# A hybrid decoder block: the first MLP product ahead of the last two norms, its operands in other room

## Chip, core and metric

The kernel runs on one core of a Trainium2 chip, as one program. The metric is the device time of an execution in microseconds. Three executions of the kernel before stand for its time, and a fourth was recorded by the profiler.

## The reference

One layer over 1024 tokens of width 1024, in float32. Its last two parts matter here:

```
x = x + concat([y_a, y_b, y_c]) @ w_out                       # three token mixers
x = x + memory_cross_attention(rms_norm(x, norm_cross), ...)  # 4 heads of 128, 256 memory rows
hm = rms_norm(x, norm_mlp) @ mlp_w1                           # 1024 -> 4096
x = x + square(relu(hm)) @ mlp_w2                             # 4096 -> 1024
```

## The kernel before

All products run on TensorE as three matmuls each: both operands are split into a high half and the rest (`split` and `split2`: a cast on ScalarE, a subtraction on VectorE), and `mm3` (L130 to L135) sums high x high (L133), high x low (L134) and low x high (L135). The program is written in order, but each engine's queue is put in order by a list scheduler that works with estimated times: an instruction that is ready by the estimate may be queued ahead of one traced before it. A queue is then fixed, and an engine runs it in that order. SP, which issues most transfers, is such a queue too. A pool hands out buffers by tag; a new tile waits for the last reader of the old tile in its bytes.

**Cross attention** runs as a software pipeline over eight tiles of 128 tokens (`for i in range(NT + 6)` in `run`): the output projection (`out_rows`, `out_b` with the tile `xr` loaded from x1_d, L1270), the norm and its transposes (`cross_h`), the query product (`cross_q`, `cross_qT`), scores and softmax (`cross_p`), values (`cross_o`), and from i = 10 `cross_w` (L1365 on), which multiplies by `wo`, adds the residual x (L1375), stores it to x3_d (L1376) and normalizes it for the MLP (square on ScalarE L1380, a ten-step reciprocal root on VectorE from L156, a multiply L196). `norm_T` transposes the normalized rows on TensorE (eight 128 x 128 transposes, L1392) and copies them into the four blocks of `h3`: `h3["gn"]` holds half g of the model width of tokens 512(n-1) to 512n-1. Tiles 4 to 7 of `cross_w` run in a loop of their own at the end, with `norm_T` two tiles behind.

**The MLP** (`mlp`) works on four groups of 1024 hidden columns. Each group has two halves, up and down, and each half is a 2 x 2 block product made from seven products instead of eight (`PRODS`, with sums of blocks from `block_sums`: S1 to S4 of the weights, T1 to T4 of the activations). A product is 4 row blocks (m) x 4 k x 3 = 48 matmuls of 128 x 512. Its weight operand `wm` is split from a raw block `wq` or a sum `wsum`, its other operand `bm` from `h3` or the sum `hsum`. In the first group `bm` is also stored to `hb_d` (L1470), and later groups load it from there. The order in the up half is 1, 2, 5, 6, 3, 7, 4. Product 1 reads w1 block "11" and `h3["11"]`, product 2 block "12" and `h3["21"]`: both are tokens 0 to 511. Product 5 needs S1 = "21" + "22" of the weights and T1 = `h3["12"]` - `h3["11"]`, so the last four tiles' norms.

What decides the order around the border of the two stages:
- `blk` has ten buffers of 8 KB per partition. It serves `xoT`, the four blocks of `h3`, the normalized rows of t = 6 and 7 (`n3y2`, one buffer), the first two raw weight blocks `wq`, `wm` of the first product, all `bm`, and later `xacc` and `am`. `blk2` has four, for other `wm`.
- The raw blocks of w1 come in 1 MB loads: two into `blk` at t = 4 (L1770), the others from the pool `mlp` (five `wq` buffers, L1479), which is opened after cross attention has closed all of its pools.
- `mlp` is a generator. `run` takes its first step (product 1 with its evictions), then `norm_T` of t = 6 and 7, then the rest.
- In the first group the weights' sums are made on GpSimd (`V if g else G`), in later groups on VectorE.
- PSUM has eight banks of 512 columns. In the cross stage four serve the query and score products (tag mg) and four the others (tag mm); `self.psum(0)` then opens a pool of eight for the MLP. A half opens four banks each for its chains ch 0, 1 and 2 (`ps[ch, m]`).
- On the right side of the memory, from the edge inwards, lie `blk2` (32 KB), `xl`, `xe`, `wr` and `xq` (called `xp` in the code); the scan and sparse attention before had there `pm` (20 KB), `woa` (42 KB) and `gdnb` (12 KB, with the scan's `oc`, stored to ya_d at L1101). `xl` holds 44 KB, `xq` 28 KB, among it `g2` and `xr`.

Of the kernel before, what the change touches and what calls it, by code (L numbers as in the profile page):

```python
# [50 lines left out]
class Block:  # L51
# [64 lines left out]
    def mm_ps(self, shape, name="mm"):  # L116
        own = self.gbanks and self.stage in ("gp", "gi", "gs", "gn", "xq", "xp")
# [1173 lines left out]
    def cross_q(self, pool, hT, wq):  # L1291
# [5 lines left out]
        qc = self.xl.tile([P, H, P], F32, name="xqc", bufs=2)  # L1297
# [7 lines left out]
    def cross_qT(self, pool, qc):  # L1305
# [4 lines left out]
        qT = [self.xl.tile([P, H, P], F32R, name=f"xqT{i}", bufs=2) for i in range(2)]  # L1310
# [28 lines left out]
    def cross_o(self, pool, Pm, v, oT, hp):  # L1339
# [5 lines left out]
        for i in range(2):  # L1345
            h = hp * 2 + i
            PT = [self.xl.tile([P, 2, 256], F32R, name=f"xPT{j}", bufs=2) for j in range(2)]
# [15 lines left out]
    def cross_w(self, x, y, t, oT, wo, g3):  # L1363
# [12 lines left out]
        nc.sync.dma_start(self.x3_d[t], x)  # L1376
# [65 lines left out]
    def mlp(self, pool, blk, h3, wq):  # L1442


        self.stage = "mlp"
# [31 lines left out]
        def raw(src):  # L1477
            t = pool.tile(bshape, F32, name="wq", bufs=5)
            nc.sync.dma_start(t, src)  # L1479
            return t  # L1480

        def new(name, tag=None):
            return lambda: early.pop(name, None) or pool.tile(bshape, F32, name=name, tag=tag or name)

        early = {"wsum": pool.tile(bshape, F32, name="wsum", tag="wsum")}

        NG = FF // GF
        for g in range(NG):

            q = dict(zip(("11", "12", "21", "22"), [raw(x) for x in self.w1_blocks(g)] if g else wq + [raw(x) for x in self.w1_blocks(0)[2:]]))  # L1490
            left = self.block_sums(V if g else G, q, {"new": new("wsum")}, False)
            right = self.block_sums(V, h3, {"new": new("hsum", "asum")}, False)
            a, ps = {}, {}
            for i, p in enumerate((1, 2, 5, 6, 3, 7, 4)):
                l, r, ch, dst = self.PRODS[p]
                l, r = half(left(l), *((blk, "blk") if g == 0 and p == 1 else ())), rows(g, i, lambda: right(r))
                for m in range(4):
# [6 lines left out]
                    for c in dst:  # L1504
                        if (c, m) not in a:
                            if m == 0:
                                a[c] = pool.tile(bshape, F32, name="aq" + c)
                            a[c, m] = x = a[c][:, m]
                            Sc.activation(x, ps[ch, m], AF.Relu if c == "21" else AF.Copy)  # L1509
                            if c == "21":  # L1510
                                V.tensor_mul(x, x, x)
                        else:
# [37 lines left out]
    def run(self):  # L1550
# [117 lines left out]
        with ExitStack() as bs:  # L1668
# [140 lines left out]
```

## Time and profile before

| | us |
|---|---|
| median of 3 executions | 1636.0 |
| lowest, highest | 1629.88, 1637.38 |
| profiled execution, its time | 1631.19 |
| span of the profiled execution | 1629.4 |
| PE busy in the span | 1508.6 (93%) |
| VectorE busy | 1171.4 (72%) |
| ScalarE busy | 739.6 (45%) |
| GpSimd busy | 318.6 (20%) |
| DMA queue on SP, share of 16 engines | 34.8% |

The span runs from the first to the last instruction in the trace; the time holds what lies around it too. PE is TensorE's matmul side, PEld its weight loads, DVE VectorE, ACT ScalarE, POOL GpSimd, SPq the queue that issues transfers. In a timeline a row gives the start, the duration, the engine, the line and the tiles written and read; in brackets stands the idle time of the engine before it and what ended that. Matmuls overlap, so the step from one start to the next, not the duration, is what one costs.

### The profile page before, as it was taken

The page shows a single profiled execution, that of the slowest core. Times are in us where ns is not written, and L with a number is a line of the kernel's source. Part 1 is how long each engine was busy: PE and PEld are TensorE (multiplying, and loading weights), DVE is VectorE, ACT ScalarE, POOL GpSimd, SP SyncE. Part 2 cuts the span into 40 slices and gives each one's busy share as a digit, 9 for nine tenths or more (in the row PEclk, how much of TensorE's full clock was granted, in tenths as well). Part 3 has the DMA queues.
Part 4 walks back from the last instruction along what each step waited for, and adds up shares of the span by engine and source line. Part 5 has one row for each costly group of instructions (what it writes and reads, how often), then busy time and mean ns, then how long its engine had stood idle before and what let it go on. Part 6 is the DMA issues. An engine that isn't in the chain of part 4 may idle for free.

```text
span 1629.4 us, 20582 instructions
## 1 busy us (share of the span) xinstructions
PE 1508.6 (93%) x7497; PEld 1256.2 (77%) x7497; DVE 1171.4 (72%) x2149; ACT 739.6 (45%) x1483; POOL 318.6 (20%) x297
## 2 busy tenths in 40 slices
PE   6999999997975789999979996999999999999999
PEld 6877788885775678888768875888888888888887
DVE  7649868678258688985767777996569656865783
ACT  4535777883541656665434542433224223323331
POOL 3021434345355333221401103100000000000000
PEclk9999999998997999999999997999999999999999
DMA  6130121221543533323712356813551364146202
GB/s 213 38 97 21 45 59 52 78 67 44 163 152 98 168 115 119 94 59 128 289 66 75 120 186 265 330 57 130 206 208 34 134 235 165 52 155 242 95 7 97
DMA packets 113811, 201.93 MB, mean 124 GB/s; under 512 B 15157, under 2 KB 64046, under 8 KB 106542
## 3 DMA queue, kind: packets, MB, share of 16 engines
q1 hardware_dynamic: 112174, 195.37, 34.8%
q0 software_dynamic: 1536, 5.24, 0.9%
q8 instruction: 59, 0.97, 0.2%
q14 instruction: 42, 0.34, 0.1%
HBM read 150.26 MB, written 50.33 MB: 123 GB/s over the span
## 4 chain that ended last, share of the span: by engine, by line
PE 65%; DVE 16%; ACT 9%; issue 5%; DMA 3%; POOL 1%; SPq 0%; ACTq 0%; DVEq 0%; POOLq 0%
PE mlp_mm L134 13%; PE mlp_mm L135 13%; PE mlp_mm L133 13%; ACT junka L588 5%; DVE acc L741 1%; PE gi_mm L1029 1%; PE xq_mm L133 1%; PE xq_mm L134 1%; PE xw_mm L135 1%; PE xw_mm L133 1%; PE xw_mm L134 1%; PE xq_mm L135 1%; DVE tk_t L596 1%; PE small_mm L135 1%; DVE junk L590 1%
## 5 line engine op out<-in xcount | busy, mean ns | idle before, releaser
L134 PE MATMUL mlp_mm<-bm,wm 128*128 128x512 f32 x448 | 178.6, 399 | 11.9 <-DVE bm L1456 11.9
L133 PE MATMUL mlp_mm<-bm,wm 128*128 128x512 f32 x448 | 178.0, 399 | 2.5 <-DVE rs_x L156 1.3
L135 PE MATMUL mlp_mm<-bm,wm 128*128 128x512 f32 x448 | 178.1, 398 | 0.0
L135 PE MATMUL mlp_mm<-wm,am 128*128 128x512 f32 x448 | 177.1, 395 | 0.0
L134 PE MATMUL mlp_mm<-wm,am 128*128 128x512 f32 x448 | 177.0, 395 | 0.0
L133 PE MATMUL mlp_mm<-wm,am 128*128 128x512 f32 x448 | 175.1, 395 | 0.0
L1455 ACT CAST wm<-wq 128x2048 fp32r<-128x2048 f32 x32 | 61.2, 1911 | 211.9 <-PE mlp_mm L134 211.7
L1545 DVE TENSOR_TENSOR xacc<-xacc,mlp_mm 128x512 f32<-128x512 f32 x112 | 75.9, 684 | 69.7 <-PE mlp_mm L135 69.7
L134 PEld LDWEIGHTS mlp_mm<-bm,wm 128*128 128x128 f32 x448 | 85.0, 190 | 33.0 <-DVE bm L1456 12.7
L133 PEld LDWEIGHTS mlp_mm<-bm,wm 128*128 128x128 f32 x448 | 85.1, 190 | 23.4 <-DVE rs_x L156 1.6
L135 PEld LDWEIGHTS mlp_mm<-bm,wm 128*128 128x128 f32 x448 | 85.1, 190 | 20.3
L133 PEld LDWEIGHTS mlp_mm<-wm,am 128*128 128x128 f32 x448 | 84.1, 188 | 20.4
L134 PEld LDWEIGHTS mlp_mm<-wm,am 128*128 128x128 f32 x448 | 84.1, 188 | 20.4
L135 PEld LDWEIGHTS mlp_mm<-wm,am 128*128 128x128 f32 x448 | 84.1, 188 | 20.3
L1456 DVE TENSOR_TENSOR wm<-wq,wm 128x2048 fp32r<-128x2048 f32 x32 | 73.3, 2291 | 28.6 <-ACT wm L1455 28.3
L1455 ACT CAST wm<-wsum 128x2048 fp32r<-128x2048 f32 x24 | 45.9, 1912 | 105.5 <-PE mlp_mm L134 79.3
L1456 DVE TENSOR_TENSOR wm<-wsum,wm 128x2048 fp32r<-128x2048 f32 x24 | 54.9, 2289 | 51.5 <-ACT wm L1455 51.5
L1509 ACT ACTIVATE aq<-mlp_mm 128x512 f32<-128x512 f32 x64 | 38.1, 595 | 72.8 <-PE mlp_mm L135 72.7
L185 POOL TENSOR_TENSOR wlo<-wraw,whi 128x1024 fp32r<-128x1024 f32 x28 | 68.5, 2445 | 1.7
L133 PE MATMUL cv_mm<-Y,diag 128*128 128x512 f32 x124 | 50.2, 405 | 11.2 <-POOL diag L784 11.2
L588 ACT ACTIVATE junka<-negm,tk_cand 128x384 bf16<-128x384 int16 (+1 forms) x68 | 52.6, 774 | 16.4 <-DVE tk_cand L597 13.7
L588 ACT ACTIVATE junka<-lo,tk_cand 128x384 bf16<-128x384 uint16 (+1 forms) x64 | 49.5, 773 | 18.5 <-DVE tk_cand L597 12.5
(515 smaller groups left out, 4092.7 us busy)
## 6 DMA issues: line engine op xcount, KB each, us to landing
bm<-hb_d SPq DMA_DIRECT2D x42, 1024.0 KB, 4.9
wq<-in_mlp_w SPq DMA_DIRECT2D x32, 1024.0 KB, 5.3
hb_d<-bm SPq DMA_DIRECT2D x14, 1024.0 KB, 4.0
wraw<-in_w_in SPq DMA_DIRECT2D x20, 512.0 KB, 4.0
qkv_d<-acc SPq DMA_DIRECT2D x12, 512.0 KB, 3.2
x<-in_x SPq DMA_DIRECT2D x8, 512.0 KB, 4.2
gnx<-qkv_d SPq DMA_DIRECT2D x8, 512.0 KB, 6.3
wraw<-in_xa_wkv SPq DMA_DIRECT2D x8, 512.0 KB, 6.0
```

The source lines that it names most:

```text
L133: mm(out, l[0], r[0], start=start, stop=False, skip_group_check=on)
L134: mm(out, l[0], r[1], start=False, stop=False, skip_group_check=on)
L135: mm(out, l[1], r[0], start=False, stop=stop, skip_group_check=on)
L185: (lo_eng or nc.gpsimd).tensor_sub(lo[:, :n], raw[:, :n], hi[:, :n].bitcast(F32))
L588: Sc.activation(junka[:, :K], X[b], AF.Sign, bias=c, scale=-1.0, accum_out=n)
L590: V.tensor_scalar(junk[:, :K].bitcast(X[b].dtype), X[b], c, None, op0=OP.is_lt, op1=OP.add, accum_out=n)
L596: V.tensor_tensor(t, cnt, th, op=OP.is_le)
L741: nc.vector.scalar_tensor_tensor(acc, xb[:, 3 - d:3 - d + T], self.cw[:, 3 - d, i:i + 1], acc, op0=OP.mult, op1=OP.add)
L1455: Sc.copy(w[0], x)
L1456: V.tensor_sub(w[1], x, w[0].bitcast(F32))
L1509: Sc.activation(x, ps[ch, m], AF.Relu if c == "21" else AF.Copy)
L1545: V.tensor_add(x, x, ps[ch, tt])
```

## The change

- `mlp` is divided so that the first step issues only the 48 matmuls of product 1; its four evictions (`evict`, L1509) come after `norm_T` of t = 6 and 7.
- The raw blocks `wq` (five buffers) and `wsum` move into a pool `mlpw` of their own on the left, opened when `xt`, `xe`, `wr` and `xq` close, which is before the last four `cross_w`. Blocks one and two are loaded there at once, ahead of these `cross_w`; blocks three and four are queued on SP behind the last x3 store. `blk` no longer holds `wq`.
- The weights' sums of the first group are made on VectorE.
- Cross attention's tiles change pools: what lives until the last norms (`xP`, `n2_y`, `g2`, `xr`) is in `xl` (36 KB), `xqT` in a new `xt` (8 KB), and `yT`, `h2T`, `xqc`, `xPT` in `xq` (28 KB).
- The four and four PSUM banks stay for the MLP: the up half takes ch 0 from mg and the others from mm, the down half ch 0 from mm and the others from mg.

```diff
-        own = self.gbanks and self.stage in ("gp", "gi", "gs", "gn", "xq", "xp")
+        own = self.gbanks and self.stage in ("gp", "gi", "gs", "gn", "xq", "xp", "mlpg")
...
-        qc = self.xl.tile([P, H, P], F32, name="xqc", bufs=2)
+        qc = self.xq.tile([P, H, P], F32, name="xqc", bufs=2)
...
-        nc.sync.dma_start(self.x3_d[t], x)
+        self.x3_store = nc.sync.dma_start(self.x3_d[t], x)
...
+        stages = ("mlpg", "mlp")
...
-            q = dict(zip(("11", "12", "21", "22"), [raw(x) for x in self.w1_blocks(g)] if g else wq + [raw(x) for x in self.w1_blocks(0)[2:]]))
-            left = self.block_sums(V if g else G, q, {"new": new("wsum")}, False)
+            q = dict(zip(("11", "12", "21", "22"), [raw(x) for x in self.w1_blocks(g)] if g else wq))
+            left = self.block_sums(V, q, {"new": new("wsum")}, False)
...
             for i, p in enumerate((1, 2, 5, 6, 3, 7, 4)):
                 l, r, ch, dst = self.PRODS[p]
+                self.stage = stages[ch > 0]
+                ahead = g == 0 and i == 0
...
-                yield 1.0
-                self.stage = "mlp"
+                    if not ahead:
+                        evict(ch, m, dst)
+                if ahead:
+                    yield 1.0
+                    for m in range(4):
+                        evict(ch, m, dst)
...
             for p in (1, 5, 6, 3, 7, 2, 4):
                 l, r, ch, dst = self.PRODS[p]
+                self.stage = stages[ch == 0]
...
+                xbs.close()
+                wpool = bs.enter_context(sb_pool(tc, "mlpw", bufs=1))
+                w1 = []
+
+                def w1_load(srcs):
+                    for src in srcs:
+                        w1.append(wpool.tile([P, 4, 512], F32, name="wq", bufs=5))
+                        nc.sync.dma_start(w1[-1], src)
+
+                w1_load(self.w1_blocks(0)[:2])
+                pools = []
+                mlp = self.mlp(wpool, pools, (blk, blk2), h3, w1)
                 for t in range(NT + 6 - W0, NT):
                     cross_w(t)
                     if t == 4:
                         h3_blocks(1)
-                        wq = [blk.tile([P, 4, 512], F32, name="wq", tag="blk") for _ in range(2)]
-                        for x, src in zip(wq, self.w1_blocks(0)):
-                            nc.sync.dma_start(x, src)
-                    if t - 2 < 6:
-                        self.norm_T(h3, t - 2, y3.pop(t - 2))
-            self.psum(0)
-            with sb_pool(tc, "mlp", bufs=1, side="right") as mp:
-                mlp = self.mlp(mp, (blk, blk2), h3, wq)
+                    self.norm_T(h3, t - 2, y3.pop(t - 2))
+                with tc.issue_after(self.x3_store.ins):
+                    w1_load(self.w1_blocks(0)[2:])
                 next(mlp)
                 for t in (6, 7):
                     self.norm_T(h3, t, y3.pop(t))
+                xas.close()
+                pools.append(xs.enter_context(sb_pool(tc, "mlp", bufs=1, side="right")))
                 self.drain(mlp)
```

## Rows read from the trace of the kernel before

**Rows 1.** Page, engines: busy us, share of the span, instructions.
```profile
PE 1508.6 (93%) x7497; PEld 1256.2 (77%) x7497; DVE 1171.4 (72%) x2149; ACT 739.6 (45%) x1483; POOL 318.6 (20%) x297
```

**Rows 2.** Waits of PE, 955 us to the end: total us, times, longest.
```profile
PE mlp_mm L134 <- DVE bm L1456: 11.9, 2, 8.7
PE n_mm L1392 <- DVE n3y L196: 2.6, 1, 2.6
PE mlp_mm L133 <- DVE rs_x L156: 1.3, 1, 1.3
PE mlp_mm L133 <- ACT bm L1455: 1.2, 1, 1.2
```

**Rows 3.** Timeline of PE at the border: start, duration, instruction [idle before, releaser].
```profile
966.19 1.03 PE L1392 MATMUL n_mm<-ident,n3y 128*128 128x128 f32 x8
966.98 0.48 PE L133 MATMUL xw_mm<-wslot,xoT 128*128 128x512 f32 x1
...
972.64 1.03 PE L1392 MATMUL n_mm<-ident,n3y 128*128 128x128 f32 x8
...
982.57 1.97 PE L1392 MATMUL n_mm<-ident,n3y 128*128 128x128 f32 x8 [2.56 <-DVE n3y L196]
993.19 0.80 PE L134 MATMUL mlp_mm<-bm,wm 128*128 128x512 f32 x1 [8.65 <-DVE bm L1456]
...
1000.01 0.39 PE L135 MATMUL mlp_mm<-bm,wm 128*128 128x512 f32 x1
...
1002.05 0.39 PE L135 MATMUL mlp_mm<-bm,wm 128*128 128x512 f32 x1
...
1009.09 0.50 PE L134 MATMUL mlp_mm<-bm,wm 128*128 128x512 f32 x1 [3.21 <-DVE bm L1456]
```

**Rows 4.** Windows: length, busy PE, PEld, DVE, ACT, POOL; clock; DMA share; GB/s.
```profile
985.00:993.20 8.20, 0.01 (x1) 0.02 (x1) 8.20 (x3) 0.00 (x0) 7.10 (x2) 0.50 1.03 381
...
1009.00:1020.00 11.00, 10.91 (x40) 8.78 (x41) 8.39 (x9) 1.91 (x1) 0.00 (x0) 0.84 0.79 323
1020.00:1080.00 60.00, 60.00 (x259) 48.66 (x259) 55.48 (x39) 27.03 (x23) 5.00 (x1) 1.00 0.68 256
```

**Rows 5.** Timeline of VectorE at the border.
```profile
981.23 1.28 DVE L196 SCALAR_TENSOR_TENSOR n3y<-x,n_y,g 128x1024 f32<-128x1024 f32 x1
...
986.55 6.58 DVE L1456 TENSOR_TENSOR bm<-h,bm 128x2048 fp32r<-128x2048 f32 x1
...
993.76 5.96 DVE L1429 TENSOR_TENSOR h<-h,h 128x2048 f32<-128x2048 f32 x1
...
1004.74 4.29 DVE L1456 TENSOR_TENSOR bm<-h,bm 128x2048 fp32r<-128x2048 f32 x1 [2.54 <-PE mlp_mm L134]
1008.96 2.28 DVE L1456 TENSOR_TENSOR bm<-hsum,bm 128x2048 fp32r<-128x2048 f32 x1
...
1027.64 9.10 DVE L1456 TENSOR_TENSOR bm<-h,bm 128x2048 fp32r<-128x2048 f32 x2
```

**Rows 6.** Timeline of ScalarE: the cast of product 1's `bm`.
```profile
972.89 1.90 ACT L1455 CAST bm<-h 128x2048 fp32r<-128x2048 f32 x1 [0.23 <-PE xw_mm L135]
```

**Rows 7.** Timeline of GpSimd: the first sum of weights.
```profile
986.02 4.96 POOL L1414 TENSOR_TENSOR wsum<-wq 128x2048 f32<-128x2048 f32 x1 [58.67 <-DMA wq<-in_mlp_w]
```

**Rows 8.** Page, groups of instructions: busy, mean ns | idle before, releaser.
```profile
L1545 DVE TENSOR_TENSOR xacc<-xacc,mlp_mm 128x512 f32<-128x512 f32 x112 | 75.9, 684 | 69.7 <-PE mlp_mm L135 69.7
```

**Rows 9.** Timeline of SP's queue: loads of weight blocks.
```profile
975.19 6.89 SPq L1479 DMA_DIRECT2D wq<-in_mlp_w  x5
```

**Rows 10.** Timelines and tile views (`ya_d`, then `xr`) at the stage's start.
```profile
782.21 0.56 POOL L1101 DMA_DIRECT2D ya_d<-oc  x1 [2.14 <-ACT oc L1100]
...
DMA to landing us min/median/max: 2.3/2.8/7.4
...
784.02 2.48 DVE L1276 TENSOR_TENSOR xr<-xr,wb_mm 128x512 f32<-128x512 f32 x4
...
DMA to landing us min/median/max: 2.8/3.2/7.6
```

More of the change, by code (lines that the diff above doesn't have):

```diff
@@ L1309, in cross_qT @@
             self.nc.tensor.transpose(pt[:, h], qc[:, h], self.ident)
-        qT = [self.xl.tile([P, H, P], F32R, name=f"xqT{i}", bufs=2) for i in range(2)]
+        qT = [self.xt.tile([P, H, P], F32R, name=f"xqT{i}", bufs=2) for i in range(2)]
         self.split(qT[0], qT[1], pt)
@@ L1346, in cross_o @@
             h = hp * 2 + i
-            PT = [self.xl.tile([P, 2, 256], F32R, name=f"xPT{j}", bufs=2) for j in range(2)]
+            PT = [self.xq.tile([P, 2, 256], F32R, name=f"xPT{j}", bufs=2) for j in range(2)]
             pt = self.mm_ps([P, 2, 256])
@@ L1440, in w1_blocks, with mlp @@
         return [w1[:, 4 * k:4 * k + 4, g * GF + j * GF // 2:g * GF + (j + 1) * GF // 2] for j in range(2) for k in range(2)]
-    def mlp(self, pool, blk, h3, wq):
-        self.stage = "mlp"
+    def mlp(self, wpool, pools, blk, h3, wq):
+        stages = ("mlpg", "mlp")
         nc, A = self.nc, self.A
@@ L1477, in raw @@
         def raw(src):
-            t = pool.tile(bshape, F32, name="wq", bufs=5)
+            t = wpool.tile(bshape, F32, name="wq", bufs=5)
             nc.sync.dma_start(t, src)
@@ L1503, in mlp @@
                                  first and k == 0, k == 3, not first)
[L1504 to L1512, printed above, removed]
-                            x = a[c, m]
-                            V.tensor_add(x, x, ps[ch, m])
-                            V.scalar_tensor_tensor(x, x, 0.0, x, op0=OP.max, op1=OP.mult)
-                yield 1.0
-                self.stage = "mlp"
+                    if not ahead:
[4 more added lines that the diff above has]
+                        evict(ch, m, dst)
             qa = {"11": a["11"], "12": a["21"], "21": a["12"], "22": a["22"]}
@@ L1686, in h3_blocks @@
                     h3[f"{g + 1}{n + 1}"] = blk.tile([P, 4, 512], F32, name="h3", tag="blk")
-            with sb_pool(tc, "xl", bufs=1, side="right") as xl, sb_pool(tc, "xe", bufs=1, side="right") as xe, \
-                    sb_pool(tc, "wr", bufs=1, side="right") as wr, \
-                    sb_pool(tc, "xq", bufs=1, side="right") as xp:
-                self.xl = xl
+            with ExitStack() as xs:
+                xas = xs.enter_context(ExitStack())
+                xl = xas.enter_context(sb_pool(tc, "xl", bufs=1, side="right"))
+                xbs = xas.enter_context(ExitStack())
+                self.xt, xe, wr, xq = (xbs.enter_context(sb_pool(tc, x, bufs=1, side="right")) for x in ("xt", "xe", "wr", "xq"))
+                xp = xl
+                self.xl, self.xq = xl, xq
                 def raw():
@@ L1727, in run @@
                     nc.gpsimd.dma_start(v[i], self.v_d[i])
+                y67 = []
                 yT, y2, h2, qc, qT, Pm = ({} for _ in range(6))
@@ L1730, in run @@
                     if i < NT:
-                        yT[i] = self.out_rows(xp, i, *rows.pop(i))
+                        yT[i] = self.out_rows(xq, i, *rows.pop(i))
                         if i + 2 < NT:
```

19 lines of the change are left out of this document (15 added, 4 removed).

## The prediction, made before the result was known

> **What bounds it now.** I read the page's busy shares first: PE holds 93% of the span [rows 1]. A change elsewhere pays only where PE stands still. The waits of PE from 955 us to the end come next: four groups, 11.9 + 2.6 + 1.3 + 1.2 = 17.0 us, and no others [rows 2]. PE's order of time puts all of them between 972.64 and 1009.09 us, at the border of cross attention and MLP [rows 3]. From 1009 on PE does not wait once, and its granted clock is 1.00 from 1020 on [rows 4]. So this border is the whole prize of the MLP side.
>
> What the border should cost follows from its own rows. Eight transposes of a norm take 966.98 - 966.19 = 0.79 us to the next instruction at full clock, and nine matmul steps from 1000.01 to 1002.05 give 0.227 us each [rows 3]. Between the two limits PE does three norms' transposes (t=5, 6, 7), the 48 matmuls of product 1, and the four of product 2 that need only high halves: 3 x 0.79 + 52 x 0.227 = 14.2 us. It takes 36.45, so 22.3 are lost. Behind the 8.65 us wait the clock row is 0.50, and the stretch from 1009 to 1020 has 10.91 us of PE work at 0.84 [rows 4]: at 2.4 GHz throughout it would be 10.91 x 0.16 = 1.7 us shorter. The prize is **24.0 us**: 17.0 of waits, the rest half-clock work (transposes of 1.97 instead of 1.03 us, the first matmuls at 0.80 [rows 3]).
>
> Why it waits: PE's 8.65 us end at the low half of `bm`, VectorE's subtraction from 986.55 that lasts 6.58 us [rows 2, 5]. `blk` has ten buffers. At product 1 they would be h3 4, the late norm rows 1, `wq` 2, `wm` 2, `bm` 2: eleven. The high half starts only at 972.89, released by the last cross matmul, whose `xoT` frees a buffer [rows 6]. The low half needs the buffer of the norm rows of t=6 and 7, read last by the transposes from 982.57 to 984.5 [rows 3]. Then `hsum` goes first, and GpSimd's addition of 4.96 us from 986.02 [rows 7] stretches the subtraction: its undisturbed length is 2.28 [rows 5].
>
> **The change, part by part.**
>
> *First product ahead.* `wq` leaves `blk`, so that nine buffers are asked for, and the tenth is `xoT`'s. `bm` for product 1 is the tile of tokens 0 to 511, complete with the norm of t=3, so before the transposes of t=4 at 966.19 [rows 3], and the earlier `xoT` are free by then. Its two casts and two subtractions (2 x 1.90 [rows 6], 2 x 2.28 [rows 5]) fit beside the last cross products. PE then goes from the transposes at 972.64 into product 1 at 973.4, ends it at 973.4 + 48 x 0.227 = 984.3, does t=6 and t=7 by 985.9 under full clock, and has product 2's four matmuls by 986.8, not 1009.09. The norm chain of t=7 (ten operations on single columns and a 1.28 us multiply [rows 5]) lies under product 1. Gross: the 24.0 above.
>
> *What is late next.* Product 2's low `bm` needs a buffer that product 1's `wm` frees at 984.3; 2.28 us give 986.6, with two copies of t=6 and 7 (0.684 each [rows 8]) perhaps ahead: 0 to 1.2 us of wait, I take 1. Products 5 and 6 need sums that need the last norms: one product lasts 10.9 us, while VectorE owes it up to two sums, two subtractions (4 x 2.28) and evictions of 4 x 2 x 0.684: 14.6. Over seven products it is 14 subtractions, 8 sums and 28 evictions, 69 us, against 76, with the tightest place at product 6; 0 to 4 us, I take 2, nearer the middle as the row of 1020 to 1080 has VectorE at 55.48 of 60 with no PE wait [rows 4]. One more for a clock that dips in such pauses (0 to 1.7).
>
> *Weights' sums on VectorE.* It adds 4 x 2.28 = 9.1 us there and takes four sums off GpSimd. The four VectorE instructions or pairs that met those sums took 6.58, 5.96, 4.29 and 9.10 (two) against 2.28 each: 4.30 + 3.68 + 2.01 + 4.54 = 14.5 us too long [rows 5]. Net VectorE gains 5.4 us; counted at nothing beyond the margins above, since PE does not wait from 1009 on.
> Against moving them: at 55.48 of 60 us VectorE has little room in this stretch [rows 4]; that is a rival below.
>
> *Loads.* The first two blocks (1 MB each) go into room where, in the new layout, `yT` and `h2T` lie, whose last use is the query product; they are traced before the last four `x` loads and stores on SP, so they can hold those up only by the time of two issues: 0. The third and fourth stand behind the last x3 store. Before, the five loads of this line left from 975.19, after that store too [rows 9], and the sum that reads them began at 986.02 [rows 7]. Product 5 needs sum, cast and subtraction by 998: 986.0 + 2.28 + 1.9 + 2.28 = 992.5, covered. With five buffers for all four w1 blocks, fewer w2 loads can run ahead; later groups live with five and PE does not wait there: 0.
>
> *Evictions.* Product 1's four copies wait for the norms; their next use is product 2's additions, 10.9 us later: 0.
>
> *Banks.* Eight shared PSUM banks become four and four for the whole MLP. The order of opening is unchanged, and each set is released one product before its next opening: 0. Upper end in the rivals.
>
> *Rooms of cross attention.* `xr` and `g2` move from the far room to `xl`, nearer the right edge, over `woa` and `gdnb`. By the sizes in the code `xr`'s first buffer covers the scan's `oc`, whose last store leaves at 782.21 and lands 2.8 us later (median); the load takes 3.2 more, hence 788.3 and a wait of its own, while the additions into `xr` run at 784.02 now [rows 10]. Cost 0 to 4.3 us at the start of the stage; other products of the output projection can fill it, so I take 2.
>
> Sum: 24.0 - 1 - 2 - 1 - 2 = **18 us**. The profiled execution took 1631.2 us (span 1629.4), which becomes 1613; the median of the three runs is 1636.0, which becomes 1618. The four times average 1633.6, and I forecast from that: 1616.
>
> **Rivals.**
>
> *The wait moves to product 2.* VectorE is in order. If the new sum stands ahead of the last norm's chain, it holds VectorE until its weights land, 986.0 [rows 7]; then come the sum (2.28), the last norm's multiply (1.28), transposes, a copy and the low half (0.79 + 0.68 + 2.28): 993.3 instead of 986.8. Gain 18 - 6.5 = 11.5, time **1622**. For: the sums now share a queue with the norms. Against: the order follows estimated readiness, and the loads are known to be late.
>
> *VectorE becomes the bound of the first group.* Products that bring two sums and evictions ask 14.6 us of it and 10.9 of PE; if the spare time of the others comes too late to help, the added 9.1 us lie on the path: gain 8.9, **1625**. For: the 55.48 of 60. Against: 14.5 us of stretching by GpSimd go at the same time [rows 5], more than comes.
> The Trainium skill (Perfetto Trace Analysis, section Optimizing Scalar/DVE Operations) speaks for this rival: where VectorE is saturated, it says, giving work to another engine, even GpSimd, may make sense, and this change takes work back. The same section adds that between these two it might not help, since they share a read port, and the stretched subtractions agree with that.
>
> *The change doesn't do it.* The norms still go ahead of product 1. Then only the stretch by GpSimd and `hsum` ahead go: low half at 984.4 to 986.6, 6.6 us less than 993.19 [rows 3, 5], less 2 for `xr`: **1629**. Against: the buffer count above.
>
> *Slower: four banks are too few.* Three products of each half open four banks, 24 openings in eight halves. If an opening waits for two additions on VectorE, each 684 ns [rows 8], it costs 1.4 us: 33 us, time 1633.6 - 18 + 33 = **1649**. It decides from 18 / 24 = 0.75 us per opening. Against: the products between release and opening last 10.9 us and evictions 4 x 1.3.
>
> **How the numbers follow.** Forecast 0.60, moved wait 0.12, VectorE bound 0.10, no effect 0.11, banks 0.07. A measurement of this kernel tells 0.5% (8.2 us) from no change: faster means below 1627.8. Faster are the forecast with 0.60, 0.11 of the moved wait and 0.08 of the VectorE case: 0.79. The rest of these two (0.03) and no effect are within: 0.14. The banks are slower: 0.07. Range: at the low end all 24 us off 1631 give 1607; at the high end it takes in the moved wait and the VectorE case with the unknowns at their upper ends, and half of no effect: 1629. The banks, the other half and a tail are left out, under 0.2.
>
> **What would show it.** Right: product 1's 48 matmuls without a break right behind the transposes at about 973; transposes of t=6 and 7 behind them near 985; PE waits after 955 of under 5 us in all; no clock below 0.9 in the border; no GpSimd sums, and VectorE subtractions of 2.28 throughout. Wrong: a PE wait of 5 us or more on `bm` of product 2 or on a sum; `xr` additions past 788 with PE idle beside them; PE waits at the openings of products in later groups.

## The result and the profile after

The changed kernel takes 1625.1 us (median of 5 runs, 1623.7 to 1630.6) against 1634.7 for the kernel before: ratio 0.9948, 95% interval [0.9924, 0.9973]. Three repeats, each on a chip of its own beside the kernel before, gave 0.9965 [0.9946, 0.9985], 0.9969 [0.9952, 0.9987] and 0.9963 [0.9945, 0.9980]. So it gains 5.4 to 9.6 us where 18 were forecast: the direction was right, the size between a third and a half.

The page of the kernel after, engines: VectorE has not grown, although four sums of 2.28 us came to it, and GpSimd has lost 21 us. Compare [rows 1].

```profile
PE 1507.9 (93%) x7497; PEld 1255.9 (77%) x7497; DVE 1167.6 (72%) x2153; ACT 739.2 (46%) x1483; POOL 297.4 (18%) x293
```

The waits of PE from 955 us to the end (total, times, longest), after. The 17.0 us of [rows 2] are 4.8 now.

```profile
PE mlpg_mm L134 <- DVE rs_x L156: 3.1, 1, 3.1
PE mlp_mm L134 <- DVE bm L1456: 0.9, 1, 0.9
PE mlpg_mm L133 <- ACT bm L1455: 0.8, 1, 0.8
```

Windows of the kernel after (length, busy PE, PEld, DVE, ACT, POOL; clock; DMA share; GB/s). They answer to [rows 4]: from 1020 PE is full at clock 1.00 as before, and the second window is at 1.00 too. The first averages 0.89: behind the wait at product 1 PE ran at 0.50 from 989.6 to 992.6.

```profile
985.00:1000.00 15.00, 11.86 (x45) 9.31 (x44) 14.02 (x19) 6.28 (x7) 0.00 (x0) 0.89 1.02 373
1000.00:1020.00 20.00, 19.10 (x90) 15.27 (x90) 19.96 (x16) 6.08 (x6) 0.00 (x0) 1.00 0.66 261
1020.00:1080.00 60.00, 60.00 (x260) 48.66 (x259) 57.41 (x44) 28.32 (x23) 0.00 (x0) 1.00 0.73 280
```

Timeline of PE at the border, after. Product 1 (`mlpg_mm`) does follow the transposes of t=5, and t=6 and 7 come behind it; but it waits twice. Product 2 at 1002.17 does not wait. Before, product 1 stood from 984.54 to 993.19 [rows 3].

```profile
982.55 1.03 PE L1392 MATMUL n_mm<-ident,n3y 128*128 128x128 f32 x8
984.43 1.19 PE L133 MATMUL mlpg_mm<-bm,wm 128*128 128x512 f32 x4 [0.84 <-ACT bm L1455]
988.76 0.50 PE L134 MATMUL mlpg_mm<-bm,wm 128*128 128x512 f32 x1 [3.14 <-DVE rs_x L156]
...
1000.51 1.91 PE L1392 MATMUL n_mm<-ident,n3y 128*128 128x128 f32 x16
1002.17 0.99 PE L133 MATMUL mlp_mm<-bm,wm 128*128 128x512 f32 x2
```

Why it waits is in two more queues of the kernel after. ScalarE casts product 1's `wm`, then product 2's `wm`, and only then product 1's `bm`; VectorE subtracts in the same order, with 2.29 us for product 2's `wm` in front of the low half of `bm` that PE wants. The row at 986.43 ends at 988.7, and there PE starts (its wait is put down to L156, the next instruction on VectorE; the one that ended it is the subtraction).

```profile
978.59 1.90 ACT L1455 CAST wm<-wq 128x2048 fp32r<-128x2048 f32 x1
980.65 1.91 ACT L1455 CAST wm<-wq 128x2048 fp32r<-128x2048 f32 x1 [0.16 <-PE xw_mm L135]
982.47 1.90 ACT L1455 CAST bm<-h 128x2048 fp32r<-128x2048 f32 x1
```
```profile
980.68 2.29 DVE L1456 TENSOR_TENSOR wm<-wq,wm 128x2048 fp32r<-128x2048 f32 x1
...
983.55 2.29 DVE L1456 TENSOR_TENSOR wm<-wq,wm 128x2048 fp32r<-128x2048 f32 x1
...
986.43 2.28 DVE L1456 TENSOR_TENSOR bm<-h,bm 128x2048 fp32r<-128x2048 f32 x1
...
993.36 2.29 DVE L1414 TENSOR_TENSOR wsum<-wq 128x2048 f32<-128x2048 f32 x1 [0.46 <-DMA wq<-in_mlp_w]
```

**Where something was lost.** The other end is the start of the cross attention, rows of the kernel after on ScalarE, GpSimd, SP, VectorE and PE. `xr` now covers the scan's `oc`. The store that reads `oc` leaves at 787.36, 0.30 us after ScalarE has filled it (785.92 to 787.06; the profile puts the store's wait down to a PE product that ended at about the same time). The two `xr` loads stand behind one another at the head of SP's queue until 790.53 (the row ahead of them is `g` at 781.18), the additions wait for them, and PE stands 5.68 us. Before, the additions ran at 784.02 [rows 10]; counted from the scan's end they come 10.4 us behind it before and 16.7 in the changed kernel. The granted clock of PE from 777.2 to 797.2 us is 0.86.

```profile
785.92 1.14 ACT L1100 ACTIVATE oc<-gs_mm,ot 128x128 f32<-128x128 f32 x4 [4.43 <-DVE ot L1098]
```
```profile
787.36 0.56 POOL L1101 DMA_DIRECT2D ya_d<-oc  x1 [4.65 <-PE wb_mm L134]
```
```profile
781.18 0.41 SPq L1724 DMA_DIRECT2D g<-in_norm_cross  x1
790.53 0.81 SPq L1270 DMA_DIRECT2D xr<-x_d  x2
```
```profile
793.85 2.58 DVE L1276 TENSOR_TENSOR xr<-xr,wb_mm 128x512 f32<-128x512 f32 x4 [2.32 <-DMA xr<-x_d]
```
```profile
794.59 1.11 PE L1257 MATMUL wb_mm<-ident,yai 128*128 128x128 f32 x4 [5.68 <-DVE xr L1276]
```

**How traces are compared from here.** The scan ahead of all this has the same instructions in the same order in both kernels, yet it ends anywhere from 773.6 to 783.3 us in the twenty profiles of these kernels, 773.6 to 779.7 in four of the kernel before. Whole spans of single profiles are therefore off by several us. I cut each trace at two instructions: stretch **A** runs from the scan's last row of matmuls (L1087, two in that row) to the last matmul of line L133 in the cross attention's output product, stretch **B** from there to the end of the span. Repeats of A and B agree within some 2 us, with one exception that turns out to matter.

| kernel | A, us | B, us | ratio to before [95%] |
|---|---|---|---|
| before, 4 profiles | 198.4, 199.6, 197.5, 198.7 | 657.5, 650.0, 656.2, 657.8 | 1 |
| b2_sums, 2 profiles | 198.4, 196.9 | 649.8, 650.0 | 0.9970 [0.9952, 0.9987] |
| e4_gpsimd | 204.9 | 647.9 | 1.0000 [0.9981, 1.0019] |
| after, 4 profiles | 204.7, 205.7, 205.7, 204.7 | 641.4, 641.6, 641.7, 641.1 | 0.9948 to 0.9969 (above) |
| e5_norms_first | 204.0 | 640.8 | 0.9978 [0.9961, 0.9995] |
| e1_rooms | 201.9 | 641.4 | 0.9947 [0.9926, 0.9968] |
| e8_rooms_first | 201.5 | 641.5 | 0.9945 [0.9924, 0.9967] |
| e2_prep | 208.1 | 638.1 | 0.9954 [0.9934, 0.9974] |
| e3_both | 204.9 | 638.7 | 0.9946 [0.9928, 0.9964] |
| e6_loads | 207.1 | 636.9 | 0.9966 [0.9950, 0.9982] |
| e10, 2 profiles | 203.7, 205.7 | 635.7, 636.0 | 0.9939 [0.9919, 0.9959], 0.9939 [0.9916, 0.9962] |
| e11_norms2 | 207.0 | 635.7 | 0.9935 [0.9917, 0.9954] |

The four profiles of after are those of the result and of a0_again, a1_again and a2_again; e10 stands for e10_after_norm and e10_again. In e2_prep, e3_both, e10 and e11_norms2 eight matmuls of product 1 (1.8 us) ran ahead of the cut and lie in A, in e6_loads 25 (5.7 us); there A+B is what can be set beside the others. By the means of four profiles each, the change adds 6.6 us to A (198.6 to 205.2) and takes 13.9 from B (655.4 to 641.5): 7.3 net, which is what the times say.

### The profile page after: what moved, and what is told of

It is laid out like the page before. It is cut to its first block, busy times and chain, and to the rows that moved or that the text cites. A ratio compares the mean times of both kernels' runs of the same rounds, so it can differ in the third digit from the quotient of the medians.

```text
span 1623.2 us, 20570 instructions
## 1 busy us (share of the span) xinstructions
PE 1507.9 (93%) x7497; PEld 1255.9 (77%) x7497; DVE 1167.6 (72%) x2153; ACT 739.2 (46%) x1483; POOL 297.4 (18%) x293
## 4 chain that ended last, share of the span: by engine, by line
PE 65%; DVE 15%; ACT 8%; issue 5%; DMA 5%; POOL 1%; SPq 0%; DVEq 0%; ACTq 0%; POOLq 0%
PE mlpg_mm L134 6%; PE mlpg_mm L135 6%; PE mlpg_mm L133 6%; PE mlp_mm L134 6%; PE mlp_mm L135 6%; PE mlp_mm L133 6%; ACT junka L588 5%; DVE acc L741 1%; DVE junk L590 1%; PE xq_mm L133 1%; PE gi_mm L1029 1%; PE xq_mm L134 1%; PE xq_mm L135 1%; PE xw_mm L135 1%; PE xw_mm L133 1%
## 5 line engine op out<-in xcount | busy, mean ns | idle before, releaser
L134 PE MATMUL mlpg_mm<-bm,wm 128*128 128x512 f32 x256 | 101.9, 398 | 3.1 <-DVE rs_x L156 3.1
L135 PE MATMUL mlpg_mm<-bm,wm 128*128 128x512 f32 x256 | 101.7, 397 | 0.0
L133 PE MATMUL mlpg_mm<-bm,wm 128*128 128x512 f32 x256 | 100.7, 397 | 0.8 <-ACT bm L1455 0.8
L135 PE MATMUL mlp_mm<-wm,am 128*128 128x512 f32 x256 | 101.1, 395 | 0.0
L134 PE MATMUL mlp_mm<-wm,am 128*128 128x512 f32 x256 | 101.1, 395 | 0.0
L133 PE MATMUL mlp_mm<-wm,am 128*128 128x512 f32 x256 | 99.2, 395 | 0.0
L1553 DVE TENSOR_TENSOR xacc<-xacc,mlp_mm 128x512 f32<-128x512 f32 x64 | 43.4, 683 | 48.9 <-PE mlp_mm L135 48.9
L134 PE MATMUL mlp_mm<-bm,wm 128*128 128x512 f32 x192 | 75.9, 395 | 0.9 <-DVE bm L1456 0.9
L133 PE MATMUL mlp_mm<-bm,wm 128*128 128x512 f32 x192 | 75.9, 396 | 0.0
L133 PE MATMUL mlpg_mm<-wm,am 128*128 128x512 f32 x192 | 75.8, 395 | 0.0
L135 PE MATMUL mlpg_mm<-wm,am 128*128 128x512 f32 x192 | 75.8, 395 | 0.0
L134 PE MATMUL mlpg_mm<-wm,am 128*128 128x512 f32 x192 | 75.8, 395 | 0.0
L135 PE MATMUL mlp_mm<-bm,wm 128*128 128x512 f32 x192 | 75.3, 395 | 0.0
L133 PE MATMUL cv_mm<-Y,diag 128*128 128x512 f32 x124 | 49.9, 403 | 11.5 <-POOL diag L784 11.5
L134 PEld LDWEIGHTS mlpg_mm<-bm,wm 128*128 128x128 f32 x256 | 48.5, 189 | 15.2 <-DVE bm L1456 3.6
L133 PEld LDWEIGHTS mlpg_mm<-bm,wm 128*128 128x128 f32 x256 | 48.3, 189 | 12.7 <-ACT bm L1455 1.1
```

The source lines that it names most:

```text
L133: mm(out, l[0], r[0], start=start, stop=False, skip_group_check=on)
L134: mm(out, l[0], r[1], start=False, stop=False, skip_group_check=on)
L135: mm(out, l[1], r[0], start=False, stop=stop, skip_group_check=on)
L1553: V.tensor_add(x, x, ps[ch, tt])
```

## Experiments

**The room of xr, and the operands of product 1.** Theory: A's loss is the load behind `oc`'s store, B's missing gain is the queue order in front of product 1. Rival: neither is on the path, and the gain went elsewhere. Four kernels on one chip, the changed one among them.

> The changed kernel as it is, as the measure for the other runs of this job. Theory (rooms and queue order): 1625 us again; in its trace PE waits about 5.7 us on the additions into xr near 794 us and some 4 us before product 1. Rival (the delay of the output projection was an accident of one execution): the wait on xr is under 2 us in this execution, with the time still near 1625.

> xP gets a pool of its own next to xt, so that g2, xr and the norm rows lie at the edge, over room of woa, and no longer over the scan's oc. Theory (the loads of xr wait for the store of oc): the 5.7 us wait of PE on xr goes, xr's first additions come some 6 us earlier against the scan's end, and the time is 1625 - 6 = 1619. Rival (the order of SP's queue delays the loads, or the pipeline's later waits absorb them): the wait on xr shrinks but the transposes of t=5 come no earlier, 1624 to 1626.

```diff
-        pm = self.xl.tile([P, H, 256], F32, name="xP", bufs=4)
+        pm = self.xm.tile([P, H, 256], F32, name="xP", bufs=4)
...
+                self.xm = xas.enter_context(sb_pool(tc, "xm", bufs=1, side="right"))
...
-                    return (xl if tag in ("xP", "n2_y") else xp).tile([P, D], F32, name=name, tag=tag, bufs=bufs)
+                    return (self.xm if tag == "xP" else xl).tile([P, D], F32, name=name, tag=tag, bufs=bufs)
```

`xP` gets a pool of its own beside `xl`, so `xr` lies nearer the edge and no longer over `oc`. 1625.7 us became 1623.7: 2.0 us where the theory had 6. The 5.5 us wait is gone and the clock from 777 to 797 us is 1.00 (0.91 in the changed kernel beside it); A falls by 3.8 against the run beside it, to 201.9, and B stays. So the mechanism is shown, and part of the gain is lost again: two short waits are left (timeline of PE in that kernel), and A is still 3.3 us above the kernel before. In the four profiles of before the first of these was 0 to 0.9 us and the second 0.6 to 1.3, 1.1 together on average; 2.7 of the 3.3 us are these two.

```profile
788.85 0.50 PE L133 MATMUL wb_mm<-wslot,yT 128*128 128x512 f32 x1 [1.53 <-DVE gz L1258]
802.39 1.09 PE L203 MATMUL xq_mm<-ident,n_y 128*128 128x128 f32 x8 [2.29 <-DVE n_y L196]
```

> The casts and subtractions of product 1's two operands are traced ahead of the cross product of t=6, the matmuls where they were. Theory (the operands were only queued too late: product 2's subtraction stood ahead of bm's on VectorE): the waits of 0.84 and 3.14 us before product 1 go, the clock stays at 1.00, the time falls by about 5.5 to 1619.6. Rival (VectorE has no room there): the additions or norms of cross attention are delayed instead and PE waits in the last cross products or at products 2 and 5, time 1624 to 1626.

```diff
+                if ahead:
+                    yield 0.5
+                    self.stage = stages[0]
+                    q.update(zip(("11", "12", "21", "22"), wq))
                 for m in range(4):
...
                 for t in range(NT + 6 - W0, NT):
+                    if t == 6:
+                        next(mlp)
                     cross_w(t)
```

The casts and subtractions of product 1 are traced ahead of `cross_w(6)`, its matmuls where they were. The 4.0 us in front of product 1 shrink to 0.9, but 2.5 us appear at product 2, and eight matmuls of product 1 slip into A. A+B is 846.2 against 847.3, the time 1625.6 us against 1625.7: the rival held, most of the wait has moved.

> Both edits together. Theory: the gains add up, 1625 - 6 - 5.5 = 1613.5, close to what the prediction gave for the change itself. Rival (one of them only moves a wait that the other also meets): 1619 or more.

Both edits: 1622.7 us, not the 1613.5 of the theory but what its rival allowed. Timelines of VectorE, then PE, of this kernel show what is late at product 2: a sum of weights stands at the head of VectorE's queue for 3.85 us until its blocks land, and the low half of product 2's `bm` is queued behind it.

```profile
994.15 2.29 DVE L1414 TENSOR_TENSOR wsum<-wq 128x2048 f32<-128x2048 f32 x1 [3.85 <-DMA wq<-in_mlp_w]
996.36 2.28 DVE L1456 TENSOR_TENSOR bm<-h,bm 128x2048 fp32r<-128x2048 f32 x1
```
```profile
998.70 0.80 PE L134 MATMUL mlp_mm<-bm,wm 128*128 128x512 f32 x1 [2.64 <-DVE bm L1456]
```

**Which part carries the gain.** Each of the two largest parts undone alone, and the kernel before profiled again.

> The changed kernel with the four weights' sums of the first group back on GpSimd. Theory: the sums cost VectorE nothing that PE feels, and on GpSimd they lengthen the subtractions of VectorE beside them again (by 2 to 4.3 us each, as before) when product 5's operands are due: PE waits of 2 to 6 us at products 5 or 6, B 643 to 647, 1627 to 1631 us. Rival (VectorE is what bounds the first group): with 9.1 us less on VectorE the 0.9 us wait at product 5 goes and nothing replaces it, B 638 to 641, 1622 to 1625 us.

```diff
-            left = self.block_sums(V, q, {"new": new("wsum")}, False)
+            left = self.block_sums(V if g else G, q, {"new": new("wsum")}, False)
```

1632.1 us, ratio 1.0000: without the sums on VectorE **nothing is left of the gain**. The theory named the direction, and the size was a little above its range (B 647.9 against 643 to 647). Rows of GpSimd, VectorE and PE: the subtraction that starts during GpSimd's sum takes 4.85 us, the low half of `bm` waits behind it on VectorE, and PE stands 4.24 us here, with a clock of 0.83 from 1000 to 1020. B is 6.4 us longer than with the change.

```profile
999.79 4.60 POOL L1426 TENSOR_TENSOR wq<-wq 128x2048 f32<-128x2048 f32 x1
```
```profile
1001.68 4.85 DVE L1456 TENSOR_TENSOR wm<-wsum,wm 128x2048 fp32r<-128x2048 f32 x1 [7.39 <-ACT wm L1455]
1006.45 2.28 DVE L1456 TENSOR_TENSOR bm<-h,bm 128x2048 fp32r<-128x2048 f32 x1
```
```profile
1008.79 0.80 PE L134 MATMUL mlp_mm<-bm,wm 128*128 128x512 f32 x1 [4.24 <-DVE bm L1456]
```

> The changed kernel with the last two norms traced ahead of the first product again: only the order is undone, operands, rooms, loads and sums stay. Theory: the norm of t=7 is ready near 990 us, so PE stands still from the transposes of t=5 (983.4) to there, 6 us in place of the 4.0 that it waits on operands, with half-clock work behind it: 2 to 5 us slower than the changed kernel, 1628 to 1631, PE waits after 940 us of 8 to 11 us. Rival (the order buys nothing, since the operands are as late as the norms): within 1 us of the changed kernel, 1625.

```diff
-                next(mlp)
                 for t in (6, 7):
                     self.norm_T(h3, t, y3.pop(t))
+                next(mlp)
```

1626.3 us, with the same two waits of 0.84 and 3.14 us at product 1, A and B as in the changed kernel: the rival holds. It is not that the order is worth nothing to PE; tracing order did not decide it. The scheduler put the start of product 1 ahead of the two norms' transposes (they run at 993.68 and 995.24 in the middle of it); in the kernel before, too, four matmuls of product 1 ran ahead of those of t=6 (from 974.85). What decides its place was not tried.

> The kernel before, unchanged, for a second profile of it. Stretch A is from the scan's last matmul (L1087) to the last matmul of the cross attention's output product (L133, xw), stretch B from there to the end of the span; the first profile had A 198.2 and B 657.5 us, and its scan ended at 773.7. Theory: the scan's end there was early by the luck of one 128x4 instruction of VectorE near 470 us (0.14 us there, 7 us in the other kernel), so an ordinary execution ends its scan at 777 to 779 us, with A 197 to 200 and B 656 to 659, span 1631 to 1635. Rival: A itself differs by 3 us or more from one execution to the next, and then the 6.5 to 7.4 us that the changed kernel loses in A are partly chance.

A was 199.6, so A's loss is no accident. The rest of that theory fell: the instruction near 470 us took 0.13 us here and the scan still ended at 779.7. And B was 650.0, 7.5 us shorter than in the profile that the prediction rests on. The row of `bm` tells why; compare [rows 5, 7]. Here GpSimd's sum begins 0.85 us **after** the low half of `bm`, which takes its 2.29 us, while the sum stretches to 5.86. In the third profile of the same kernel (the last two rows) it begins 0.11 us before, and the subtraction takes 6.58.

```profile
993.44 5.86 POOL L1414 TENSOR_TENSOR wsum<-wq 128x2048 f32<-128x2048 f32 x1 [58.60 <-DMA wq<-in_mlp_w]
```
```profile
992.59 2.29 DVE L1456 TENSOR_TENSOR bm<-h,bm 128x2048 fp32r<-128x2048 f32 x1
```
```profile
987.59 4.55 POOL L1414 TENSOR_TENSOR wsum<-wq 128x2048 f32<-128x2048 f32 x1 [58.62 <-DMA wq<-in_mlp_w]
```
```profile
987.70 6.58 DVE L1456 TENSOR_TENSOR bm<-h,bm 128x2048 fp32r<-128x2048 f32 x1
```

The subtraction ends 2.14 us behind the end of the sum (987.70 + 6.58 against 987.59 + 4.55): it stands until the sum is through and then runs about its usual length. In b1_before three later VectorE instructions beside the sums took 5.94, 5.63 and 6.70 us, and B was 650.0 all the same, as short as with no sum on GpSimd at all (b2_sums, below): of the stretches in this kernel, only the one at product 1's `bm` shows in B. The sum's start hangs on when weights land, the subtraction's on the norms; which comes first differs between executions.

> A third profile of the kernel before. Theory (the border differs between executions, since it hangs on when the first weights land and GpSimd's sum starts beside the low half of bm): B anywhere from 649 to 658, A 198 to 200; the first sum's start relative to the low half of bm (0.53 us before it in the first profile, 0.85 us after it in the second) tells which. Rival: B is 650 nearly always and the first profile was the one odd execution.

> A fourth profile of the kernel before, with the same expectations: if GpSimd's first sum starts before the low half of bm, that subtraction takes 6 us or more and B is 655 to 658; if it starts after, the subtraction takes 2.3 and B is 649 to 652.

Both had the sum first (by 0.11 and 0.13 us), both subtractions took 6.58 us, and B was 656.2 and 657.8. So three of four profiles of the kernel before fall in the long case.

> The kernel before with one edit: the four weights' sums of the first group on VectorE. Theory 1 (the sums are what the gain rests on, and the rooms only lose): stretch A stays at 198 to 200 us, the low halves of bm are no longer lengthened, B falls from 650 to 657.5 to 645 to 648, and with it the time to 1626 to 1629 us, most or all of the changed kernel's gain. Theory 2 (the order is needed too): VectorE now does two sums and a subtraction between product 1's and product 2's low half, the wait at product 2 becomes 5 us or more, B stays at 650 or above, 1631 to 1634 us.

```diff
-            left = self.block_sums(V if g else G, q, {"new": new("wsum")}, False)
+            left = self.block_sums(V, q, {"new": new("wsum")}, False)
```

This one line in the kernel **before** gives 1627.5 us, beside 1627.9 for the whole change on that chip: the same gain, 0.9970 against 0.9969 (the sums alone were set beside the change on this one chip). B was 649.8, a little above the first theory's 645 to 648, and A as before.

> The kernel before with the sums on VectorE, a second profile. Theory: with no sum on GpSimd the low half of bm takes 2.29 us whenever the weights land, so B stays at 649 to 651 as in its first profile. Rival: B moves by 3 us or more here too, and something other than GpSimd's sums makes the border differ.

B 650.0 again. Without a sum on GpSimd the low half of `bm` takes 2.28 us, and the long case did not come up in either profile.

> The changed kernel, unchanged, as the yardstick on the same chip for the two that follow: 1625 to 1627 us, A 204.5 to 206, B 641 to 642, PE waits after 940 us of 4 to 7 us.

> The changed kernel with the xr rooms mended and the last two norms traced ahead of the first product again. Theory (the order is worth nothing, the rooms cost 3 to 4 us): A 201 to 202, B 640 to 642, 2 to 4 us faster than the changed kernel on this chip, 1622 to 1624 us. Rival (the order is worth something that the one run without it hid): 1625 us or more, with PE waits at the transposes of the last two norms.

With the room mended and the norms traced first: 1624.1 us, A 201.5. A falls as in e1_rooms, and again the order of tracing changes nothing.

**A version that beats both.** First the four weight blocks all loaded ahead, on top of e3_both:

> Rooms and early operands both mended (as in the run of both), and all four weight blocks loaded ahead of the last cross products instead of two behind the last x3 store. Theory: what is left at product 2 is VectorE standing 3.85 us at a sum whose weights have not landed, with the low half of bm queued behind it (994.15, then 996.36); with the blocks there early, the 2.6 us wait of PE at product 2 goes: B 634 to 636 from 638.7, 1619 to 1621 us from 1622.7. Rival: the low half of bm waits for its buffer or for the second norm, not for the sum; the wait stays at 2 us or more and the time at 1622 to 1623.

```diff
-                w1_load(self.w1_blocks(0)[:2])
+                w1_load(self.w1_blocks(0))
...
-                with tc.issue_after(self.x3_store.ins):
-                    w1_load(self.w1_blocks(0)[2:])
```

A miss: 1624.5 us, and A+B is 844.0 against 843.6 for e3_both. The wait at product 2 went, and one of 7.08 us came at the transposes of the last norm. With the weights there early, the scheduler puts a low half of `bm` and a sum into VectorE's queue between the first and the second instruction of the norm of t=7 (989.22 and 993.69), which then ends at 997.2, where it ended at 990.3 in e3_both. So the later loads of the change are what keeps the sums behind the norms. Rows of VectorE, then PE, of this kernel:

```profile
991.48 2.29 DVE L1419 TENSOR_TENSOR wsum<-wsum,wq 128x2048 f32<-128x2048 f32 x1
...
995.88 1.28 DVE L196 SCALAR_TENSOR_TENSOR n3y<-x,n_y,g 128x1024 f32<-128x1024 f32 x1
```
```profile
997.31 1.94 PE L1392 MATMUL n_mm<-ident,n3y 128*128 128x128 f32 x8 [7.08 <-DVE n3y L196]
```

So the next kernel loads blocks three and four one tile earlier and ties the sums behind the last norm in VectorE's queue:

> The kernel with both mended (rooms, early operands), the third and fourth weight blocks loaded one token tile earlier, and the weights' sums kept behind the last norm in VectorE's queue. Theory: the sum no longer waits for its weights (3.85 us there), the low half of bm of product 2 comes 3 us earlier and PE's wait of 2.6 us there goes, while the norm of t=7 is not delayed as it was with the loads early and the order free: PE waits after 940 us below 2 us in all, B 634 to 636, A 204 to 205, A+B 839 to 841, ratio to the kernel before 0.992 to 0.994, about 1620 us. Rival: the low half waits for a buffer that product 1 reads to its end; then 2 us of wait stay and the ratio is 0.9945 as without it.

```diff
+                    if t == 7:
+                        with tc.issue_after(self.x3_store.ins):
+                            w1_load(self.w1_blocks(0)[2:])
                     cross_w(t)
...
-                with tc.issue_after(self.x3_store.ins):
-                    w1_load(self.w1_blocks(0)[2:])
...
-        self.norm_rows(y, x, self.rsqrt(ss, 1, 1.0 / D, EPS, "n3"), g3)
+        self.n3_last = self.norm_rows(y, x, self.rsqrt(ss, 1, 1.0 / D, EPS, "n3"), g3)
...
+                with (self.tc.issue_after(self.n3_last.ins) if g == 0 and l[0] == "S" else nullcontext()):
+                    wl = left(l)
```

It is e3_both with these edits (`norm_rows` returns its instruction). PE's waits after 940 us are one group, and VectorE has norm, sums and the low half without a pause between 992.89 and 1000.9:

```profile
PE mlp_mm L134 <- DVE bm L1456: 2.3, 2, 1.7
```
```profile
992.89 1.28 DVE L196 SCALAR_TENSOR_TENSOR n3y<-x,n_y,g 128x1024 f32<-128x1024 f32 x1
994.10 2.28 DVE L1414 TENSOR_TENSOR wsum<-wq 128x2048 f32<-128x2048 f32 x1
996.41 2.29 DVE L1426 TENSOR_TENSOR wq<-wq 128x2048 f32<-128x2048 f32 x1
998.62 2.28 DVE L1456 TENSOR_TENSOR bm<-h,bm 128x2048 fp32r<-128x2048 f32 x1
```

B is 635.7, A+B 839.4 and the time 1620.7 us, as the theory had it; the waits of 2.3 us are a little above the 2 that it allowed.

> The changed kernel as the yardstick on this chip: 1625 to 1628 us, A 204.5 to 206, B 641 to 642.

> The repaired kernel of the run before (rooms, early operands, weights one tile earlier, sums behind the last norm), beside the changed kernel on one chip. Theory: its A+B was 839.4 against 846.1 to 847.5, so it is 5 to 8 us faster than the changed kernel here: 1618 to 1622 us. Rival: the gain in the border is within what a profile moves, and the two lie within 3 us.

On one chip 1622.3 us (seven runs, 1617.7 to 1625.3) against 1625.8 for the change (twelve, 1624.1 to 1631.0): 3.5 us faster, less than the theory's 5 to 8 and hardly more than the rival's 3; A+B differs by 4.1. The repaired kernel beats the kernel before in both runs, by 0.61%; its intervals and the change's overlap, though five of its seven runs on this chip lie below the fastest of the change's twelve: its lead over the change is likely, and small.

> The repaired kernel, with the second tile's norm of the cross attention's start kept behind the first's in VectorE's queue. Theory (the rest of A's loss is that order): the first norm is done some 3 us earlier, PE's 2.28 us wait at its transposes falls below 0.5, A goes from 203.7 to 201 to 202, the time 1 to 3 us below the repaired kernel on this chip. Rival: the second norm is then what PE waits for, A stays at 203 or above and the time is the same.

```diff
-        y, r = self.rms_rows(self.xl, x, "n2", bufs=2)
-        self.norm_rows(y, x, r, g2)
+        with (self.tc.issue_after(self.n2_last.ins) if t == 1 else nullcontext()):
+            y, r = self.rms_rows(self.xl, x, "n2", bufs=2)
+            self.n2_last = self.norm_rows(y, x, r, g2)
```

A miss: 1622.1 us, A 207.0. The wait of 2.28 us at the first norm's transposes is still there, and a second one of 2.47 came, since the next instruction on VectorE now holds for a late `gz` row (2.81 us) with the second norm behind it. The first norm was not helped, for another reason than its place in the queue: one 128x1 instruction of its chain, 0.15 us long elsewhere, stands beside GpSimd's subtraction for `wslot` and ends 0.02 us after it. Rows of GpSimd, then VectorE, of this kernel:

```profile
796.55 2.38 POOL L1209 TENSOR_TENSOR wslot<-wraw,wslot 128x1024 fp32r<-128x1024 f32 x1
```
```profile
796.63 2.32 DVE L162 SCALAR_TENSOR_TENSOR rs_t<-rs_t,rs_x 128x1 f32<-128x1 f32 x1
```

The same chain was held for as long in the kernel before (2.32 us at 787.61), and taking that subtraction off GpSimd was not tried. So why these waits are longer than before, and with that the last 3 us of A's loss, stays open.

## Why the prediction was right or wrong, point by point

**The prize was read right, for three executions of four.** The waits and the half clock at the border are on the path, and the repaired kernel shows that the border can be had: its B of 635.7 and the 1.8 us of product 1 that lie in its A make 637.5, where the forecast (657.5 - 20) wanted 637.5. But the long border hangs on a race: in one profile of before out of four the subtraction came first, and the border was short; by the mean of four, B is 655.4, so 2.1 us of the prize were not there to be won on average.

**The first step that failed is "its two casts and two subtractions fit beside the last cross products".** There was time and room for them (e2_prep has the two casts of product 1 at 965.86 and 974.70, ahead of its last cross products), but in the change each engine's queue had another order: product 2's `wm` ahead of product 1's `bm` on ScalarE and VectorE. PE went from the transposes not into product 1 but into waits of 0.84 and 3.14 us. The margins taken for later places (1 at product 2, 2 at products 5 and 6, 1 for the clock) came out as 0, 0.9 and 1.3 (11.86 us of work at a clock of 0.89), so B came out at 641.4 where 637.5 was forecast. Of these 3.9 us the rows give 2.2 (0.84 + 3.14 + 0.9 + 1.3 against the 4 allowed); the rest is not in any one row.

**The second is the term of the `xr` rooms: 2 us with an upper end of 4.3, measured 6.6.** The mechanism was right, down to the store and the wait of the additions; the size was not. The 2 stood on other products of the output projection filling the wait: they filled it until 788.9, and then PE stood 5.68 us. The upper end took the store's time from before, 782.21 [rows 10], 8.6 us behind the scan's end. In the changed kernel the store left 10.2 us behind it, since `oc` was filled later; from the store to the loads it took 3.2 us and from the loads to the additions 3.3, near the 2.8 and 3.2 of the forecast; and the pause brought a lower clock. Of the 6.6 us the new room is 3.8 (e1_rooms), and most of the rest are the two waits shown there, whose cause was not settled.

**The third is "counted at nothing" for the sums.** The prediction had the pieces: 14.5 us of stretching and the 6.58 us row. It booked the stretch at product 1's `bm` under the order, as part of what the first product ahead would win, and left nothing for the sums. That does not move the forecast's sum, only what the gain is credited to, and that it had wrong. Undone alone they cost 6.4 us of B (e4_gpsimd); done alone they bring the whole measured gain (b2_sums). The rest of the change is a trade: from b2_sums to the change B falls by 8.4 and A rises by 7.5.

Together the rooms (6.6 against 2), product 1 and what follows it (3.9) and the race (2.1) take 10.6 from the 18 and leave 7.4; A and B give 7.3.

**The rivals.** The wait that moves to product 2, behind a sum whose weights have not landed, did not happen in the change (0.46 us at 993.36, after the norm). A milder form came in e2_prep and e3_both: the sum stood behind the last norm but ahead of product 2's low half, and held VectorE 3.72 and 3.85 us until its weights landed. e6_loads showed its other face, the sum ahead of the norm. VectorE as the bound of the first group: it is full from 1000 to 1020 (19.96 of 20 us) and costs 0.9 us, no more; taking the sums off it made the kernel slower by 6.4 us of B, so this rival is out. That its time, 1625, is the one measured is chance. The Trainium skill (Perfetto Trace Analysis, Optimizing Scalar/DVE Operations) would consider GpSimd for work of a saturated VectorE; e4_gpsimd speaks against that here. Its warning in the same place, that the two share a read port, agrees with the 6.58 us rows. The rival that the change does not do what it says is out by the timeline: t=6 and 7 stand behind product 1. Four banks: no PE wait from 1016 to the end, so out.

**What would show it.** PE waits after 955 of under 5 us: right (4.8). VectorE's subtractions of 2.28 throughout and no sums on GpSimd: right. Product 1 without a break, and no clock below 0.9: wrong (two waits, and 0.89 in the first window). The second sign named for a wrong forecast, `xr` additions past 788 with PE idle beside them, came true at 793.85, which is 790.3 if the scan's end, 3.5 us later here, is taken off.

## What to carry to other kernels

Before a stall is put down to the order of the work, take the one instruction that ended last and see whether it had its usual length; if another engine's instruction beside it made it long, the cheapest edit is to move that one, and here one line did as much as the whole change. Room and an early load do not put an operand's casts ahead in an in-order queue: name what else is traced for the same engines just before, and tie the urgent one in front (or the patient one behind). And profile the kernel before more than once when the gain is near 1%: one of its four executions had a border 7 us shorter than the others.

## What the runs showed of the hardware that was not expected

A VectorE instruction of 128x4 elements can take 7 us. Near 470 us the row was 0.14 us in the kernel before and 7.03 in the changed one, ending 0.04 us after the last of a run of GpSimd instructions; nothing of the change lies there. One GpSimd instruction was still running when it started, and the others followed without a pause. In the kernel before GpSimd paused at this place for 0.90 us. Timeline of VectorE before, of GpSimd before, of VectorE after, and of GpSimd after:

```profile
470.73 0.14 DVE L156 TENSOR_SCALAR rs_x<-kss 128x4 f32<-128x4 f32 x1
```
```profile
471.66 1.04 POOL L184 TENSOR_SCALAR whi<-wraw 128x1024 fp32r<-128x1024 f32 x1 [0.90 <-DMA wraw<-in_xa_wkv]
```
```profile
470.37 7.03 DVE L156 TENSOR_SCALAR rs_x<-kss 128x4 f32<-128x4 f32 x1
```
```profile
469.78 0.62 POOL L945 TENSOR_SCALAR_AFFINE_SELECT qkT<-E 128x512 f32<-128x512 f32 x1
470.39 1.03 POOL L184 TENSOR_SCALAR whi<-wraw 128x1024 fp32r<-128x1024 f32 x1
...
476.74 0.62 POOL L945 TENSOR_SCALAR_AFFINE_SELECT qkT<-E 128x512 f32<-128x512 f32 x1
```

By these rows a run of GpSimd instructions, one right behind the other, can hold a VectorE instruction until the run ends; the 6.58 us of `bm` are the same with one sum. It is no rule: in the twenty profiles this instruction took 7.0 us four times, some 3.6 us five times and 0.13 to 0.14 us eleven times, and in b1_before the next ones of its chain each went through between two GpSimd instructions (0.90 and 1.20 us). Whether this moves the scan's end was not tried: executions with 0.14 us here ended it as late.
